# Shifted copies by small tile products and two heads' scores in the row halves of the array, in a ten-stage decoder kernel

## The chip, the cores and the metric

The kernel runs on one core of a Trainium2 chip. The metric is the device time in microseconds of one execution; the time before is the median of three runs. The profile is one further execution. TensorE (PE in the rows; PEld are its loads of weights), VectorE (DVE), ScalarE (ACT) and GpSimd (POOL) compute; SyncE (SP) only issues DMAs here. ScalarE issues a few DMAs too (ACTq in the rows).

## What is computed

256 tokens of 1024 features pass through four layers: a layer of two convolution mixers, a stick-breaking attention layer, each followed by a layer of 32 experts (top 2), and two layers of a second block (ab and nsa attention, a softmax with a bias by distance, each followed by a gated feed-forward and a small gated projection). What the change touches is cut out here:

```
g = b_val * sigmoid(b_gate)                     # 256 tokens x 512 channels
g = causal_depthwise_conv(g, conv_b_w)          # 31 taps, each channel on its own

z = einsum("bhqd,bhkd->bhqk", qb, kb) * scale   # 16 heads of 64, stick-breaking
log_keep = where(causal, log_sigmoid(-z), 0.0)
later = cumsum(log_keep, reverse=True) - log_keep
a = where(causal, exp(log_sigmoid(z) + later), 0.0)

s = einsum('bhqd,bhkd->bhqk', q, k) * ATTN_SCALE + bias   # ab and nsa, 16 heads of 64
p = softmax(where(mask, s, -inf));  o = p @ v
```

## The kernel before

One Python function writes all engines' programs in order; the order in the code is the order in each engine's queue. `later(n, f)` puts a piece of work `f` off by n ticks, and `tick()`, called after each half of a weight item, runs what is due. So attention work is strewn between the dense products.

Weights come as items of 1 MB through a stream of buffers: `pump` issues the next load on SP (L202) whenever a buffer is free, and `done` frees one. A dense product works in three float32r products (`mm3`, L397 to L399), for which each half of an item is split into a high part `wh` (ScalarE, L237) and a low part `wl` (VectorE, L248). A half of a `feat_unit` is 24 such products of 256 columns. The expert stages read their weights unsplit (L893, L915); they are 192 items each.

`conv_mix` is the first stage. It makes `gp` (two blocks of 128 channels, tokens along the row, with 30 zeros ahead), once per half i of the 512 channels. The 31-tap convolution is done by TensorE: row group s (32 rows) of `gs` holds the same 32 channels as the others, shifted by s tokens, so one product applies four taps, and eight products (q) of 32 output columns cover the taps. Four chunks c of 32 channels stand in the four column groups. `shifted(i)` makes `gs` from `gp` by a write to DRAM and four reads with a row offset, all issued by ScalarE (L607, L609). `conv(0)` follows the dense products of i = 1; `shifted(1)` comes directly behind it, and `conv(1)` after two more units.

In the stick-breaking stage a group of four heads is handled as two pairs m. `qz` holds the two heads of a pair in two planes r: plane 0 has head 0's 64 rows and zeros below, plane 1 zeros and head 1's rows, so one product with the pair's 128 rows of keys gives one head's scores. `scores` (L1126 to L1129; the helper `zmm` gives all of them line L1117) adds a causal mask by a product with an identity, `sums` adds the reversed cumulative sums by products with `ntri` and `nones`, `values` (L1167, L1170) multiplies by the values, 64 output columns per head. The ab stage (L1444, L1445) and the nsa stage (L1779, L1780, L1791, L1792) use such planes too, written by `put_q`. In nsa the product of the compressed values `vc` is L1808, 32 rows and 64 output columns per head.

Of the kernel before, what the change touches and what calls it, by code (L numbers as in the profile page):

```python
# [10 lines left out]
F32 = mybir.dt.float32  # L11
F32R = mybir.dt.float32r
# [8 lines left out]
SEQ = 256  # L21
# [49 lines left out]
def tile_kernel(ctx: ExitStack, tc: tile.TileContext, A, out, first=0, last=9):  # L71
# [468 lines left out]
    def conv_mix():  # L540


        with tc.tile_pool(name="cm", bufs=1, reuse_waits="tile") as cp:
# [84 lines left out]
            for i in range(2):  # L628
# [7 lines left out]
                shifted(i)  # L636
# [427 lines left out]
    def stick_mix():  # L1064
        with tc.tile_pool(name="st", bufs=1, reuse_waits="tile") as cp, \
# [14 lines left out]
            qz = cp.tile([128, 2, 2, SEQ], F32, name="qz")  # L1080
            G.memset(qz, 0.0)
# [37 lines left out]
            def attn(hg, qt, kt, vt):  # L1119
                st = {}  # L1120

                def scores(m):
                    z0, z1 = bank(), bank()
                    z0v = z0.rearrange("p (r t) -> p r t", r=2)
                    z1v = z1[:, 0:256].rearrange("p (r t) -> p r t", r=2)
                    zmm(z0v, kt[:, m, 0:128], qt[:, m], start=True)  # L1126
                    zmm(z0v[:, :, 0:128], identb, negb[:, None, :].to_broadcast([128, 2, 128]))
                    zmm(z1v, kt[:, m, 128:256], qt[:, m, :, 128:256], start=True)
                    zmm(z1v, identb, negb[:, None, :].to_broadcast([128, 2, 128]))  # L1129
                    sp = cw.tile([128, 768], F32, name="sp", bufs=3)  # L1130
                    for z, a, n in ((z0, 0, 512), (z1, 512, 256)):
                        S.activation(sp[:, a:a + n], z[:, 0:n], AF.Abs)
                    S.activation(sp, sp, AF.Exp, scale=-1.0)
                    S.activation(sp, sp, AF.Ln, bias=ones_t[:, 0:1])
                    for z, a, n in ((z0, 0, 512), (z1, 512, 256)):
                        V.scalar_tensor_tensor(sp[:, a:a + n], z[:, 0:n], 0.0, sp[:, a:a + n], op0=OP.max, op1=OP.add)
                    st[m] = (z0, z1, sp)

                def parts(m):
                    sp = st[m][2]  # L1140
                    sh = cw.tile([128, 768], F32R, name="sh")
                    S.activation(sh, sp, AF.Copy)
                    sl = cw.tile([128, 768], F32R, name="sl", tag="sp", bufs=3)
                    V.tensor_tensor(out=sl, in0=sp, in1=sh.bitcast(F32), op=OP.subtract)
                    st[m] = st[m][:2] + (sh, sl)

                def sums(m):
                    z0, z1, sh, sl = st[m]
                    z0v = z0.rearrange("p (r t) -> p r t", r=2)
# [5 lines left out]
                    a = cw.tile([128, 768], F32, name="a", tag="sp", bufs=3)  # L1155
                    S.activation(a[:, 0:512], z0, AF.Exp)
                    S.activation(a[:, 512:768], z1[:, 0:256], AF.Exp)
                    st[m] = a

                def values(m):  # L1160
                    a = st[m]
                    po = bank()
                    for i in range(2):
                        for r in range(2):
                            f = slice(m * 128 + r * 64, m * 128 + r * 64 + 64)
                            if i == 0:
                                T.matmul(po[64 * r:64 * r + 64, 0:256], vt[:, 0, f], a[:, r * 256:(r + 1) * 256],  # L1167
                                         start=True, stop=False)
                            else:
                                T.matmul(po[64 * r:64 * r + 64, 128:256], vt[:, 1, f],  # L1170
                                         a[:, 512 + r * 128:640 + r * 128], start=False, stop=True)
# [843 lines left out]
```

## Time and profile before

| | us |
|---|---|
| median of three runs | 1948.1 (1944.86 to 1948.65) |
| profiled execution | 1949.69 |
| its span | 1948.0 |
| TensorE busy in the span | 1646.1 (84%) |
| weight loads of TensorE busy | 1241.9 (64%) |
| VectorE busy | 741.1 (38%) |
| ScalarE busy | 676.2 (35%) |
| GpSimd busy | 125.7 (6%) |

The shares are means over stages with different limits, so the table alone names no bound. The stages, in the order of time, are conv (0 to about 150 us), experts (to 600), stick (to 731), experts (to 1190), ab (to about 1320), feed-forward and projection (to 1556), nsa (to 1716) and the second feed-forward and projection (to the end).

### The profile page before, as it was taken

How to read it: one execution, taken by the hardware profiler on the slowest of the kernel's cores; microseconds unless marked ns; L12 is line 12 of the kernel's file. 1: busy time of each engine (PE TensorE's matmuls, PEld its weight loads, DVE VectorE, ACT ScalarE, POOL GpSimd, SP SyncE). 2: the span in 40 equal slices, each digit the busy share in tenths (PEclk: the TensorE clock that was granted, in tenths of full speed). 3: DMA queues.
4: the chain of work that ended last, by engine and by line, in shares of the span. 5: the costliest groups of instructions: out<-in, count | busy, mean ns of one | idle time of the engine just before them, and what ended most of it. 6: DMA issues, size and time to landing. Idle time of an engine off the chain costs nothing. (4 is left out here: it accounts for less than half of the span.)

```text
span 1948.0 us, 34920 instructions
## 1 busy us (share of the span) xinstructions
PE 1646.1 (84%) x14941; PEld 1241.9 (64%) x14941; DVE 741.1 (38%) x1495; ACT 676.2 (35%) x1289; POOL 125.7 (6%) x130
## 2 busy tenths in 40 slices
PE   6799767668669999767658768999999998999998
PEld 6686323224226886323324235999999997799998
DVE  4163100001104663100001104666655857666557
ACT  3143112111114663211111114665444646654445
POOL 0001000000001000000000002111000412110002
PEclk9899877768788999878777788999999999999999
DMA  9659999999999649999999998545555463145550
GB/s 280 240 208 396 418 418 418 419 419 418 418 419 347 244 173 374 418 420 419 418 419 419 418 418 304 167 151 179 184 183 175 139 207 112 55 136 195 192 177 22
DMA packets 239033, 561.95 MB, mean 288 GB/s; under 512 B 15723, under 2 KB 127146, under 8 KB 238872
## 3 DMA queue, kind: packets, MB, share of 16 engines
q1 hardware_dynamic: 226520, 551.59, 74.3%
q10 hardware_dynamic: 11728, 7.88, 1.6%
q8 instruction: 120, 1.97, 0.4%
q14 instruction: 41, 0.34, 0.0%
q0 software_dynamic: 624, 0.18, 0.0%
HBM read 557.87 MB, written 1.74 MB: 287 GB/s over the span
## 5 line engine op out<-in xcount | busy, mean ns | idle before, releaser
L893 PE MATMUL ps<-w,xg 128*32 128x256 f32 x4096 | 365.7, 498 | 233.1 <-DMA w<-in_expert_w_up_dram 228.3
L893 PEld LDWEIGHTS ps<-w,xg 128*32 128x32 f32 x4096 | 136.4, 132 | 443.1 <-DMA w<-in_expert_w_up_dram 259.5
L248 DVE TENSOR_TENSOR wl<-w,wh 128x1024 fp32r<-128x1024 f32 x255 | 310.3, 1228 | 184.2 <-ACT wh L237 180.9
L237 ACT ACTIVATE wh<-w 128x1024 fp32r<-128x1024 f32 x273 | 282.9, 1051 | 102.2 <-PE ps L398 60.1
L897 DVE TENSOR_TENSOR hs<-hs,ps 128x128 f32<-128x128 f32 x64 | 18.4, 288 | 632.3 <-ACT hs L896 632.3
L397 PE MATMUL ps<-xh,wh 128*128 128x256 f32 (+1 forms) x840 | 237.5, 283 | 0.0
L399 PE MATMUL ps<-xh,wl 128*128 128x256 f32 (+1 forms) x840 | 236.7, 282 | 0.8 <-DVE wl L248 0.8
L398 PE MATMUL ps<-xl,wh 128*128 128x256 f32 (+1 forms) x840 | 236.9, 282 | 0.4 <-DVE xl L1219 0.3
L896 ACT ACTIVATE hs<-ps 128x128 f32<-128x128 f32 x64 | 17.7, 277 | 591.7 <-PE ps L893 587.1
L399 PEld LDWEIGHTS ps<-xh,wl 128*128 128x128 f32 (+1 forms) x840 | 159.4, 190 | 1.2 <-DVE wl L248 1.2
L398 PEld LDWEIGHTS ps<-xl,wh 128*128 128x128 f32 (+1 forms) x840 | 159.4, 190 | 1.2 <-DVE xl L1219 1.2
L397 PEld LDWEIGHTS ps<-xh,wh 128*128 128x128 f32 (+1 forms) x840 | 159.4, 190 | 0.0
L915 PE MATMUL ps<-w,ht 128*32 128x256 f32 x2048 | 145.3, 433 | 0.0
L922 ACT ACTIVATE y<-ps 32x256 f32<-32x256 f32 x256 | 95.8, 374 | 121.5 <-PE ps L915 114.2
L915 PEld LDWEIGHTS ps<-w,ht 128*32 128x32 f32 x2048 | 75.0, 129 | 68.8 <-issue 38.0
L399 PE MATMUL ps<-wh,xl 128*128 128x256 f32 x352 | 100.8, 286 | 5.0 <-DVE xl L1219 5.0
L248 POOL TENSOR_TENSOR wl<-w,wh 128x1024 fp32r<-128x1024 f32 x18 | 43.4, 2417 | 948.8 <-ACT wh L237 948.8
L397 PE MATMUL ps<-wh,xh 128*128 128x256 f32 x352 | 102.5, 291 | 1.5 <-ACT xh L1216 1.5
L398 PE MATMUL ps<-wl,xh 128*128 128x256 f32 x352 | 99.7, 283 | 0.0
L398 PE MATMUL ps<-al,wh 128*128 128x256 f32 x352 | 99.2, 282 | 0.0
L397 PE MATMUL ps<-ah,wh 128*128 128x256 f32 x352 | 99.2, 282 | 0.0
L399 PE MATMUL ps<-ah,wl 128*128 128x256 f32 x352 | 99.1, 282 | 0.0
(406 smaller groups left out, 2809.6 us busy)
## 6 DMA issues: line engine op xcount, KB each, us to landing
w<-in_expert_w_up_dram SPq DMA_DIRECT2D x256, 1024.0 KB, 17.9
w<-in_expert_w_down_dram SPq DMA_DIRECT2D x128, 1024.0 KB, 18.3
w<-in_w_ffn_gate_dram SPq DMA_DIRECT2D x22, 1024.0 KB, 5.7
w<-in_w_ffn_up_dram SPq DMA_DIRECT2D x22, 1024.0 KB, 5.3
w<-in_w_ffn_down_dram SPq DMA_DIRECT2D x22, 1024.0 KB, 4.9
w<-in_odd_w_qkv_dram SPq DMA_DIRECT2D x12, 1024.0 KB, 11.6
w<-in_w_in_ab_dram SPq DMA_DIRECT2D x12, 1024.0 KB, 9.5
w<-in_w_in_nsa_dram SPq DMA_DIRECT2D x10, 1024.0 KB, 5.3
```

The source lines that it names most:

```text
L237: S.activation(hv, src, AF.Copy)
L248: eng.tensor_tensor(out=lv, in0=src, in1=hv.bitcast(F32), op=OP.subtract)
L397: T.matmul(ps, lh, rh, start=start, stop=False, **kw)
L398: T.matmul(ps, lh, rl, start=False, stop=False, **kw)
L399: T.matmul(ps, ll, rh, start=False, stop=stop, **kw)
L893: T.matmul(pu[32 * j:32 * j + 32, 0:256], r, w[:, kk, :, j, :], start=k == 0, stop=k == 7)
L896: S.activation(hs, pu[:, 0:128], AF.Silu)
L897: V.tensor_tensor(out=hs, in0=hs, in1=pu[:, 128:256], op=OP.mult)
L915: T.matmul(pd[32 * c:32 * c + 32, 0:256], hts[e][:, 32 * j:32 * j + 32], w[:, jj, c * 256:(c + 1) * 256], start=j == 0, stop=j == 3)
L922: S.activation(y4s[q][32 * ee:32 * ee + 32, c * 256:(c + 1) * 256], pd[32 * c:32 * c + 32, 0:256], AF.Copy)
```

## The change

`shifted` no longer goes through DRAM. Per block b of 128 channels, 16 products of 32 rows and 32 output columns with a 32x32 block of the identity move each 32-channel chunk c into each row group s of a bank of its own, shifted by s columns; four copies, two on ScalarE and two on VectorE, then bring the banks to `gs`. The first call is put off by one tick.

The scores of the two heads of a pair are made with 64 rows each: head 0 in rows 0 to 63 of the array, head 1 in rows 64 to 127, with outputs in two banks. `qz` and its memsets go; `qt` holds queries without zeros, and each engine writes 256 columns on 128 partitions in place of 512 on 64. In the stick stage the two banks are now one per head, so masks, sums and activations are cut 384 + 384 in place of 512 + 256.

```diff
-            def shifted(i):
-                t = dram.tile([128, 2, 32 + SEQ], F32, name=f"shifts{i}")
-                S.dma_start(t, gp)
-                for s in range(4):
-                    S.dma_start(gs[32 * s:32 * s + 32], t.rearrange("(c f) b u -> f b c u", c=4)[:, :, :, s:s + 28 + SEQ])
+            def shifted():
+
+                for b in range(2):
+                    ps = [bank()[:, 0:28 + SEQ] for _ in range(4)]
+                    for s in range(4):
+                        for c in range(4):
+                            f = slice(32 * c, 32 * c + 32)
+                            T.matmul(ps[c][32 * s:32 * s + 32], ident[f, f], gp[f, b, s:s + 28 + SEQ], start=True,
+                                     stop=True)
+                    for c in range(4):
+                        if c % 2:
+                            S.activation(gs[:, b, c, :], ps[c], AF.Copy)
+                        else:
+                            V.tensor_copy(gs[:, b, c, :], ps[c])
...
                 if i:
                     conv(0)
-                shifted(i)
+                    shifted()
+                else:
+                    later(1, shifted)
...
-                    z0, z1 = bank(), bank()
-                    z0v = z0.rearrange("p (r t) -> p r t", r=2)
-                    z1v = z1[:, 0:256].rearrange("p (r t) -> p r t", r=2)
-                    zmm(z0v, kt[:, m, 0:128], qt[:, m], start=True)
-                    zmm(z0v[:, :, 0:128], identb, negb[:, None, :].to_broadcast([128, 2, 128]))
-                    zmm(z1v, kt[:, m, 128:256], qt[:, m, :, 128:256], start=True)
-                    zmm(z1v, identb, negb[:, None, :].to_broadcast([128, 2, 128]))
...
+                    zs = [bank()[:, 0:384] for _ in range(2)]
+                    for lo in (0, 128):
+                        for r in range(2):
+                            q = slice(64 * r, 64 * r + 64)
+                            zmm(zs[r][:, 256:384] if lo else zs[r][:, 0:256], kt[q, m, lo:lo + 128], qt[q, m, lo:],
+                                start=not lo)
+                    for z in zs:
+                        zmm(z.rearrange("p (a t) -> p a t", a=3)[:, 0:3:2], identb,
+                            negb[:, None, :].to_broadcast([128, 2, 128]))
...
-                    for v in (sh, sl):
-                        zmm(z0, ntri, v[:, 0:512])
-                        zmm(z0v[:, :, 128:256], nones, v[:, 512:768].rearrange("p (r t) -> p r t", r=2),
-                            stop=v is not sh)
-                        zmm(z1[:, 0:256], ntri, v[:, 512:768], stop=v is not sh)
...
+                    for r in range(2):
+                        for v in (sh, sl):
+                            zmm(zs[r][:, 128:256], nones, v[:, r, 256:384])
+                            zmm(zs[r], ntri, v[:, r], stop=v is not sh)
...
+    def put_q(qt, ps, gcol):
+
+        S.activation(qt[:, 0, :], ps[:, 0], AF.Copy, scale=qgain[:, gcol:gcol + 1])
+        V.tensor_scalar(qt[:, 1, :], ps[:, 1], qgain[:, gcol:gcol + 1], None, op0=OP.mult)
+
+    def two_heads(qt, kt, n):
+
+
+        bk = [bank(), bank()]
+        for a, lo in ((0, 0), (n, 128)):
+            for r in range(2):
+                q = slice(64 * r, 64 * r + 64)
+                T.matmul(bk[r][:, a:a + n - lo], qt[q, 0:128] if lo else qt[q, 128:256], kt[q, lo:n],
+                         start=True, stop=True)
+        return bk
```

ScalarE's queue in the convolution stage, from the tap rows to the copies of conv(0), before (names as in the text; `scr` takes conv's result; line numbers of after are shifted by the change):

```order
L596 ACTIVATE wv<-vec 32x4x7 x2
L237 ACTIVATE wh<-w 128x1024 x2
L607 DMA shifts_366<-gp 128x576
L609 DMA gs<-shifts_366 32x8x284 x4
L237 ACTIVATE wh<-w 128x1024 x2
L631 ACTIVATE sg<-ps 128x512
L237 ACTIVATE wh<-w 128x1024 x2
L619 ACTIVATE scr<-ps,vec 128x256 x2
L607 DMA shifts_561<-gp 128x576
L609 DMA gs<-shifts_561 32x8x284 x4
```

The same stretch of ScalarE's queue now:

```order
L596 ACTIVATE wv<-vec 32x4x7 x2
L237 ACTIVATE wh<-w 128x1024 x2
L616 ACTIVATE gs<-ps 128x284 x4
L237 ACTIVATE wh<-w 128x1024 x2
L640 ACTIVATE sg<-ps 128x512
L237 ACTIVATE wh<-w 128x1024 x2
L628 ACTIVATE scr<-ps,vec 128x256 x2
L616 ACTIVATE gs<-ps 128x284 x4
```

Where five DMA issues stood, four copies out of TensorE's banks stand, and the splits behind them wait for those.

TensorE's queue at the first call of scores in the ab stage, before (`kT` are the keys of a pair, `qz` its queries in two planes; the dense products stand on both sides):

```order
L399 MATMUL ps<-wh,xl 128x256
L1444 MATMUL ps<-kT,qz 128x256
L1445 MATMUL ps<-kT,qz 128x128
L1444 MATMUL ps<-kT,qz 128x256
L1445 MATMUL ps<-kT,qz 128x128
L397 MATMUL ps<-wh,xh 128x256
```

The same place of TensorE's queue now:

```order
L399 MATMUL ps<-wh,xl 128x256
L1375 MATMUL ps<-kT,qt 128x256 x2
L1375 MATMUL ps<-kT,qt 128x128 x2
L397 MATMUL ps<-wh,xh 128x256
```

The two heads' products of equal length now stand next to each other, in two row halves; their number is the same.

TensorE's queue at the sums of a pair in the stick stage, now (`sh` and `sl` are the two parts of the softplus; before there were six products, of 512, 256 and 256 columns twice):

```order
L1126 MATMUL ps<-sh,none 128x128
L1126 MATMUL ps<-sh,ntri 128x384
L1126 MATMUL ps<-sl,none 128x128
L1126 MATMUL ps<-sl,ntri 128x384
L1126 MATMUL ps<-sh,none 128x128
L1126 MATMUL ps<-sh,ntri 128x384
L1126 MATMUL ps<-sl,none 128x128
L1126 MATMUL ps<-sl,ntri 128x384
```

There are eight products, four per head, with the same columns in all.

## Rows read from the trace of the kernel before

**Rows 1.** Windows by stage: length; busy PE, PEld, DVE, ACT, POOL; clock; DMA share, GB/s.
```profile
150.00:600.00 450.00, 326.14 (x3489) 155.63 (x3489) 45.90 (x150) 73.60 (x199) 6.03 (x11) 0.81 1.02 414
600.00:731.00 131.00, 128.08 (x940) 111.00 (x939) 82.73 (x113) 78.48 (x117) 8.67 (x13) 1.00 0.69 240
...
1210.00:1330.00 120.00, 118.83 (x969) 113.14 (x969) 82.17 (x208) 70.20 (x152) 16.62 (x12) 1.00 0.48 149
1556.00:1716.00 160.00, 150.14 (x1140) 132.45 (x1140) 101.11 (x367) 90.16 (x238) 36.66 (x27) 0.97 0.38 121
```
**Rows 2.** Waits of TensorE, 0 to 130 us: us in total, times, longest.
```profile
PE ps L616 <- DMA gs<-shifts: 10.6, 2, 7.8
```
**Rows 3.** Timeline of ScalarE: start, length, engine, line, operation, count, [idle before].
```profile
29.04 0.35 ACTq L607 DMA_DIRECT2D shifts<-gp  x1
34.90 2.68 ACTq L609 DMA_DIRECT2D gs<-shifts  x4
37.68 2.00 ACT L237 ACTIVATE wh<-w 128x1024 fp32r<-128x1024 f32 x2 [13.68 <-issue]
```
**Rows 4.** Timeline of TensorE's products, 34 to 92 us.
```profile
34.63 0.27 PE L399 MATMUL ps<-w,wl 128*128 128x256 f32 x1
38.79 0.53 PE L397 MATMUL ps<-w,wh 128*128 128x256 f32 x1 [3.88 <-ACT wh L237]
...
47.99 1.07 PE L616 MATMUL ps<-gs,w 128*32 128x256 f32 x16 [2.88 <-DMA gs<-shifts]
...
56.72 0.38 PE L397 MATMUL ps<-w,wh 128*128 128x256 f32 x1
...
66.00 0.28 PE L399 MATMUL ps<-w,wl 128*128 128x256 f32 x1
...
82.01 1.08 PE L616 MATMUL ps<-gs,w 128*32 128x256 f32 x8 [7.76 <-DMA gs<-shifts]
...
91.32 0.39 PE L397 MATMUL ps<-w,wh 128*128 128x256 f32 x1
```
**Rows 5.** Windows within conv(1): length, busy PE, granted clock, DMA share, GB/s.
```profile
82.00:86.60 4.60, 4.59 (x44) 0.50 0.05 20
87.00:91.00 4.00, 4.00 (x81) 1.00 0.00 0
```
**Rows 6.** Waits of SP's DMA queue, 0 to 170 us, the longest.
```profile
SPq L202 <- DVE wl L248: 63.6, 9, 27.4
```
**Rows 7.** Timeline of TensorE around the value products of a pair, stick stage.
```profile
652.53 0.28 PE L399 MATMUL ps<-wh,w 128*128 128x256 f32 x1
652.74 0.65 PE L1167 MATMUL ps<-a,vt 128*64 128x256 f32 x4
653.22 0.39 PE L1170 MATMUL ps<-a,vt 128*64 128x128 f32 x4
...
653.76 0.28 PE L398 MATMUL ps<-w,wh 128*128 128x256 f32 x1
```
**Rows 8.** Timeline of TensorE, first half of a pair's sums, stick stage.
```profile
645.11 0.40 PE L1117 MATMUL ps<-sh,ntri 128*128 128x512 f32 x1
645.34 0.28 PE L1117 MATMUL ps<-sh,none 128*128 128x256 f32 x1
645.46 0.28 PE L1117 MATMUL ps<-sh,ntri 128*128 128x256 f32 x1
```
**Rows 9.** Timeline of TensorE around a pair's scores, ab stage.
```profile
1227.47 0.59 PE L1444 MATMUL ps<-kT,qz 128*128 128x256 f32 x2
1227.90 0.38 PE L1445 MATMUL ps<-kT,qz 128*128 128x128 f32 x2
...
1228.89 0.28 PE L398 MATMUL ps<-wl,xh 128*128 128x256 f32 x1
```
**Rows 10.** Timeline of TensorE, a pair's product with the compressed values, nsa stage.
```profile
1670.80 0.65 PE L1808 MATMUL ps<-pct,vc 32*64 32x256 f32 x4
```
**Rows 11.** Chain of work that ended last, products of one column.
```profile
1558.27 1.24 PE ps L1238 x12
```

More of the change, by code (lines that the diff above doesn't have):

```diff
@@ L1155, in sums @@
-                    a = cw.tile([128, 768], F32, name="a", tag="sp", bufs=3)
-                    S.activation(a[:, 0:512], z0, AF.Exp)
-                    S.activation(a[:, 512:768], z1[:, 0:256], AF.Exp)
+                    zs, sh, sl = st[m]
+                    for r in range(2):
+                        for v in (sh, sl):
+                            zmm(zs[r][:, 128:256], nones, v[:, r, 256:384])
+                            zmm(zs[r], ntri, v[:, r], stop=v is not sh)
+                    a = cw.tile([128, 2, 384], F32, name="a", tag="sp", bufs=3)
@@ L1158, in sums @@
+                    for r in range(2):
+                        S.activation(a[:, r], zs[r], AF.Exp)
                     st[m] = a
@@ L1351, in turn_heads @@
         return ps.rearrange("p (m t) -> p m t", m=2)
-    def put_q(qz, ps, gcol):
-        S.activation(qz[0:64, :, 0, :], ps[0:64], AF.Copy, scale=qgain[0:64, gcol:gcol + 1])
-        V.tensor_scalar(qz[64:128, :, 1, :], ps[64:128], qgain[64:128, gcol:gcol + 1], None, op0=OP.mult)
+    def put_q(qt, ps, gcol):
[4 more added lines that the diff above has]
+        for a, lo in ((0, 0), (n, 128)):
+            for r in range(2):
+                q = slice(64 * r, 64 * r + 64)
+                T.matmul(bk[r][:, a:a + n - lo], qt[q, 0:128] if lo else qt[q, 128:256], kt[q, lo:n],
+                         start=True, stop=True)
+        return bk
     def scaled_values(pool, ps, r, name, **kw):
@@ L1431, in ab_mix @@
                 tc.tile_pool(name="abw", bufs=2, reuse_waits="tile") as cw:
-            qz = cp.tile([128, 2, 2, SEQ], F32, name="qz")
-            G.memset(qz, 0.0)
+            qt = cp.tile([128, 2, SEQ], F32, name="qt")
             yh = bp.tile([128, 8, SEQ], F32R, name="yh", tag="qh")
@@ L1440, in scores @@
                     def scores(m=m):
-                        bk = []
-                        for r in range(2):
-                            sc = bank()
-                            T.matmul(sc[:, 0:256], qz[:, m, r, 128:256], kt[:, m, :], start=True, stop=True)
-                            T.matmul(sc[:, 256:384], qz[:, m, r, 0:128], kt[:, m, 128:256], start=True, stop=True)
-                            bk.append(sc)
-                        return bk
+                        return two_heads(qt[:, m, :], kt[:, m, :], 256)
                     def values(p, m=m):
@@ L1474, in turn_q @@
                 def turn_q(qn=qn, dil=dil):
-                    put_q(qz, turn_heads(qn, jdent, False), dil)
+                    put_q(qt, turn_heads(qn, jdent, False), dil)
                 later(4 if not hg else 3, turn_q)
@@ L1615, in nsa_mix @@
             pos, w2, b1, b2 = [sl[n] for n in ("pos", "w2", "b1", "b2")]
-            qz = [cp.tile([128, 2, 2, SEQ], F32, name=f"qz{i}") for i in range(2)]
-            for i in range(2):
-                G.memset(qz[i], 0.0)
+            qts = [cp.tile([128, 2, SEQ], F32, name=f"qt{i}") for i in range(2)]
             xh, xl = cur.h, cur.l
@@ L1763, in plan @@
             def plan(g, bias):
-                qt = qz[g % 2]
+                qt = qts[g % 2]
                 f = slice(g * 64, (g + 1) * 64)
@@ L1787, in win @@
                 def win(m):
-                    bk = []
-                    for r in range(2):
-                        sc = bank()
-                        T.matmul(sc[:, 0:256], qt[:, m, r, 128:256], kwt[:, g, :], start=True, stop=True)
-                        T.matmul(sc[:, 256:384], qt[:, m, r, 0:128], kwt[:, g, 128:256], start=True, stop=True)
-                        bk.append(sc)
+                    bk = two_heads(qt[:, m, :], kwt[:, g, :], 256)
                     if m == 0:
@@ L1855, in q_unit @@
                 qn, qs = head_norm(cw, tok_unit(xh, xl), cur, "qn")
-                return qs, lambda: put_q(qz[g % 2], turn_heads(qn, jdent, False), 2)
+                return qs, lambda: put_q(qts[g % 2], turn_heads(qn, jdent, False), 2)
             gate_unit()
```

43 lines of the change are left out of this document (16 added, 27 removed).

## The prediction

> **What bounds the kernel now.** I read the stages first, in the table of windows [rows 1]. The two expert stages are bound by the stream of weights: in 150 to 600 us the 16 DMA engines are busy all the time (share 1.02) while TensorE is busy 326 of 450 us. The three attention stages are bound by TensorE: 128.1 of 131 us busy in the stick-breaking stage (600 to 731), 118.8 of 120 in the ab stage, 150.1 of 160 in the nsa stage, with DMA shares of 0.69, 0.48 and 0.38. So whatever TensorE saves there moves the end, except where a wait already follows it.
>
> The convolution stage (0 to 150 us) is different, and I read it in three views: who TensorE waited for, the order of ScalarE's queue, and TensorE's timeline. TensorE waited 10.6 us in two places for the shifted copies `gs` [rows 2]. ScalarE's queue shows why more than that is lost [rows 3]. The write of `shifts` is issued at 29.04, the four reads of it only at 34.90 to 37.58, since they wait for the write to land, and they are issued by ScalarE: its next split of weights (L237) runs at 37.68, after 13.68 us in which it did nothing. TensorE's timeline [rows 4] has the consequence: the last product of a half at 34.63, the next only at 38.79; conv(0) starts at 47.99; conv(1) starts at 82.01, after 7.76 us of idle time. After such gaps the granted clock is low: 0.50 (the 1.2 GHz level) during the first half of conv(1), 1.00 during the second [rows 5].
>
> **Does time saved there reach the end?** The expert stage behind it is bound by its weights, so the question is what holds the weight stream before. SP's own waits in 0 to 170 us are mostly for `wl` of L248 (63.6 us in 9 waits) [rows 6]: it waits for buffers that the convolution stage has not yet used up. The stream is thus held by TensorE's progress, and if the stage ends X earlier, buffers come free X earlier, the stream becomes continuous X earlier, and the expert stage ends X earlier. I count X in full.
>
> **Part 1, the shifted copies.** Removed: five DMA issues per call of `shifted`, two calls, on ScalarE's queue; with them the round trip through DRAM. SP's queue loses nothing, but shares the DMA engines with them. Added: per call 32 products of 32x32 tiles over 284 columns on TensorE, four copies on ScalarE and four on VectorE. Moved: the first call by one tick, behind the first half of the next `feat_unit` (about 29 us), where `gp` is just written.
>
> What remains between 34.75 (34.63 and one product) and 91.32 when nothing waits: one half of 24 products at 0.117 us each (645.34 to 645.46, [rows 8]), 2.8 us; conv(0); the run from 56.72 to 66.12, 9.4 us, which never waited; another half, 2.8 us; conv(1). A conv at full clock is worth 7.0 us: 82.01 to 91.32 is 9.31 us, of which 4.65 up to 86.66 at half clock count as 2.3 [rows 4, 5]. Sum 2.8 + 7.0 + 9.4 + 2.8 + 7.0 = 29.0 us of 56.6, so 27.6 us are waits and low clock that the removal can give back.
>
> The new products are priced by bounds, since nothing in the trace runs sixteen tiles. conv's own products go four at a time: 64 of them in 7.0 us, 0.109 us each for 256 columns [rows 4, 5]; 32 of 284 columns would be 32 x 0.109 x 284/256 = 3.9 us a call. Sixteen at a time would be 1.0 us. The two products of `vc` (L1808) differ in row group and in column group, and their four passes lie within 0.65 us [rows 10], where one 256-column float32 product alone takes 0.43 us (1227.47 to 1227.90, [rows 9]): row groups do run together. I take 2.0 us a call, eight at a time, 4.0 us in all. By the Trainium skill (TensorE: Matmul & The Clock Gate, Measured speedup vs the span model) sixteen 32x32 tiles were 10.6 times as fast as one after the other; an estimate from that page is 1.5 us a call, and the sum would be 1 us lower. No row of this trace shows sixteen tiles.
>
> Cover of the rest: the eight copies of a call, shared by two engines, lie beside `feat_unit` in the first call and beside four halves (12 us) in the second; without that cover they would cost their own length, some 2 us a call. The first call waits for `gp`, written just before 29.04 [rows 3]; TensorE is there 48 products ahead of 34.75, at 29.1, so it waits 0.1 us or less. Next late is nothing that I see: of the two splits at 37.68 the first is of weights that TensorE wanted at 34.75, and ScalarE can make it as soon as its copies are done, at about 31. **Part 1: -27.6 + 4.0 = -23.6 us.**
>
> **Part 2, two heads in the row halves.** 32 calls of scores: 8 in stick, 8 in ab, 16 in nsa. Before, a call's products (256, 128, 256, 128 columns, heads padded with zeros to 128 rows) go one after the other: from 1227.47 to the normal pace behind (1228.89 less 0.12) 1.30 us [rows 9]. After, the same columns stand as two pairs. The trace has such pairs in other halves of the array: the value products L1167 and L1170, 64 output columns each, 256 + 128 columns per head. Between the normal pace ahead (652.65) and behind (653.76 less 0.12) they take 0.99 us [rows 7], though the columns of one head alone would be 0.64; the rest is the change of tile shape on both sides. So I take 0.31 us off per call. Bounds: 0.66 off if the switch costs nothing; 0.35 more than before if the pairs do not overlap and the switch is paid.
>
> The loads of weights may bind instead: a call still loads eight times, 128 columns wide, where the value products load 64. The row nearest to a bare load is L1238, 12 products of one column in 1.24 us [rows 11], 0.10 us each; eight in a line and the switch are 0.83 + 0.35 = 1.18 us, 0.12 off a call, and the sum 4 to 5 us higher, inside my range. The Trainium skill (TensorE: Matmul & The Clock Gate, LDWEIGHTS (loading the stationary operand)) speaks for that price: a load's time goes with its columns and not with its rows, so half-height loads save nothing. No row here shows a half-height load.
>
> Stick, per call of `sums`: 6 float32r products become 8, with the same 2048 columns. Before: 0.23, 0.12, 0.12 twice, 0.93 us [rows 8]. After: four of 384 columns (0.175) and four of 128. For 128 no row exists: half of 0.12 if columns count, 0.10 by the loads of [rows 11], 0.21 if such a short one goes at the float32 pace of [rows 9]. I take 0.10: 1.10 us, 0.17 more; the bounds are 0.0 and 0.6 more. Stick: 8 x (-0.31 + 0.17) = -1.1 us. Ab: 8 x -0.31 = -2.5 us. Nsa: 16 x -0.31 = -5.0 us, but TensorE already idles some 10 us there [rows 1], so part of what it saves only lengthens a wait for the softmax; I count half, -2.5 us. `put_q` writes half as many columns per engine, hidden by TensorE in stick and ab; the removed memsets are on GpSimd, which nobody waits for. **Part 2: -6.1 us.**
>
> **Sum.** -23.6 - 6.1 = -29.7. The profiled execution took 1949.7 us (span 1948.0), 1.6 more than the median 1948.1, so it becomes 1920.0 and the median **1918.4 us**.
>
> **Rivals.** (a) *Row groups do not run together; only column groups do.* Then a call of scores costs 0.35 more, `shifted` 3.9 a call: 27.6 - 7.8 = 19.8 won, 8 x 0.35 + 8 x (0.35 + 0.17) + 16 x 0.35 / 2 = 9.8 lost, 1938 us. For it: no row shows products that differ in row group alone. Against: L1808 [rows 10]. (b) *The tile products go one at a time,* in the order written, since neighbours share a column group: 64 x 0.109 x 4 x 284/256 = 31 us of TensorE in place of 27.6 us of waits, and the heads' 10 us: 1948 + 3 + 10 = 1961 us, **slower**. It decides from 0.43 us a product on (64 x 0.43 = 27.6). Against: conv itself overlaps four. (c) *The convolution stage's gain is swallowed by the weight stream:* the expert stage ends when the last weight lands, and if the stream were held by something other than buffers, only part 2 would be left: 1942 us. For it: share 1.02 from 150 us on. Against: SP waits for buffers [rows 6].
>
> **How the numbers follow.** Forecast 0.82, (a) 0.08, (b) 0.05, (c) 0.05. Within the forecast the low end takes sixteen tiles at a time (-25.6) and a free switch (8 x -0.66 twice and half of 16 x -0.66, -16): 1906. The high end takes four at a time (-19.8), the loads' price (0.12 off a call) and the dear 128-column products (8 x 0.6 more), +2: 1930. So 1906 to 1931, which leaves the three rivals out, 0.18. About 0.2% (4 us) is what a measurement of this kernel can tell from no change. Faster by more: forecast, (a) and (c), less a little for a mix of bad cases, 0.94; same 0.01; slower 0.05.
>
> **What would show it.** Right: no wait of TensorE for `gs`, no gap at 35 to 39 us, granted clock 1.00 from 12 us to the expert stage; conv(1) ending near 68 us; the products of `shifted` in about 2 us a call; the expert stage starting and ending some 24 us earlier with the same length; a call of scores in 1.0 us. Wrong: tile products whose starts lie 0.1 us or more apart; a longer first expert stage; new idle time in front of conv(1), where VectorE's copies stand ahead of its splits; `sums` well over 1.1 us.

## The result, and the profile after

The changed kernel takes **1918.97 us** (median of 4 runs, 1918.88 to 1923.46), the kernel before 1947.8 us beside it (4 runs, 1944.86 to 1948.65): a ratio of 0.9867, 95% interval 0.9852 to 0.9881 (the quotient of the two medians is 0.9852, at its lower end). The forecast was 1918.4 us. The profiled execution took 1918.91 us. Its page begins (span; busy time, share and instructions by engine):

```profile
span 1917.3 us, 35268 instructions
PE 1631.0 (85%) x15117; PEld 1228.9 (64%) x15117; DVE 738.6 (39%) x1503; ACT 676.8 (35%) x1297; POOL 122.0 (6%) x126
```

**Where the time went.** Some products stand at a border between stages in both kernels. Here they are in the trace of after (TensorE's timeline: start, length, engine, line, operation, count, idle before):

```profile
68.13 0.38 PE L397 MATMUL ps<-w,wh 128*128 128x256 f32 x1
...
580.63 0.33 PE L507 MATMUL ps<-ident,x 128*128 128x128 f32 x1 [0.49 <-DVE x L495]
...
704.65 0.38 PE L507 MATMUL ps<-ident,x 128*128 128x128 f32 x2
...
1165.42 0.33 PE L507 MATMUL ps<-ident,xn 128*128 128x128 f32 x1 [0.24 <-DVE xn L495]
...
1304.75 0.28 PE L1248 MATMUL ps<-ones_t,sq 128*128 128x1 f32 x2
...
1529.40 0.42 PE L1248 MATMUL ps<-ones_t,sq 128*128 128x1 f32 x2
...
1682.09 0.43 PE L1811 MATMUL ps<-pct,vc 32*64 32x256 f32 x2
```

The same products stand at 91.32 [rows 4], 605.60, 731.28, 1193.08, 1333.32, 1558.11 and 1713.55 us in the trace before. The differences, and what each stretch adds:

| up to the end of | before | after | earlier by | gained in the stretch |
|---|---|---|---|---|
| conv(1) | 91.32 | 68.13 | 23.2 | 23.2 |
| first expert stage | 605.60 | 580.63 | 25.0 | 1.8 |
| stick-breaking stage | 731.28 | 704.65 | 26.6 | 1.7 |
| second expert stage | 1193.08 | 1165.42 | 27.7 | 1.0 |
| ab stage | 1333.32 | 1304.75 | 28.6 | 0.9 |
| feed-forward between | 1558.11 | 1529.40 | 28.7 | 0.1 |
| nsa stage | 1713.55 | 1682.09 | 31.5 | 2.8 |
| span | 1948.0 | 1917.3 | 30.7 | -0.8 |

**The convolution stage.** Around the two calls of `shifted` and behind conv(1) TensorE's timeline reads:

```profile
29.29 2.18 PE L612 MATMUL ps<-gp,ident 32*32 32x284 f32 x64
...
31.40 0.39 PE L397 MATMUL ps<-w,wh 128*128 128x256 f32 x1
...
47.13 1.78 PE L612 MATMUL ps<-gp,ident 32*32 32x284 f32 x64
48.84 0.39 PE L397 MATMUL ps<-w,wh 128*128 128x256 f32 x1
...
67.80 0.40 PE L625 MATMUL ps<-gs,w 128*32 128x256 f32 x4
```

A call holds TensorE for 2.1 us (29.29 to 31.40) and 1.7 us; each float32 product is recorded as two passes, so 64 records are 32 products. As far as it has begun by 29.395 us, the first call reads:

```profile
29.29 0.52 PE L612 MATMUL ps<-gp,ident 32*32 32x284 f32 x16
```

Nothing of [rows 2] or of the gaps in [rows 4] is left. The granted clock in the two halves of conv(1), 0.50 and 1.00 in [rows 5] (columns as in [rows 1]):

```profile
61.00:64.50 3.50, 3.50 (x66) 2.11 (x68) 2.36 (x5) 0.91 (x2) 0.00 (x0) 1.00 1.03 405
64.50:68.20 3.70, 3.70 (x73) 2.02 (x61) 0.00 (x0) 0.00 (x0) 0.00 (x0) 1.00 0.91 363
```

ScalarE's queue, where [rows 3] showed 13.68 us without work, now has the copies (L616) and two splits of weights behind them:

```profile
30.26 0.71 ACT L616 ACTIVATE gs<-ps 128x284 f32<-128x284 f32 x2 [6.16 <-PE ps L612]
31.61 0.71 ACT L616 ACTIVATE gs<-ps 128x284 f32<-128x284 f32 x2 [0.64 <-PE ps L612]
32.20 2.00 ACT L237 ACTIVATE wh<-w 128x1024 fp32r<-128x1024 f32 x2
```

**The attention stages.** A call of scores in the ab stage, against [rows 9]:

```profile
1199.91 0.28 PE L399 MATMUL ps<-wh,xl 128*128 128x256 f32 x1
1200.12 0.92 PE L1375 MATMUL ps<-kT,qt 64*128 64x256 f32 x8
1200.97 0.39 PE L397 MATMUL ps<-wh,xh 128*128 128x256 f32 x1
1201.19 0.28 PE L398 MATMUL ps<-wl,xh 128*128 128x256 f32 x1
```

From the normal pace ahead (1199.91 + 0.12) to the normal pace behind (1201.19 - 0.12) it is 1.04 us in place of 1.30. The stick stage's sums, against [rows 8], come in four pairs of 128 and 384 columns:

```profile
619.45 0.22 PE L1126 MATMUL ps<-sh,none 128*128 128x128 f32 x1
619.51 0.39 PE L1126 MATMUL ps<-sh,ntri 128*128 128x384 f32 x1
619.74 0.22 PE L1126 MATMUL ps<-sl,none 128*128 128x128 f32 x1
...
620.60 0.28 PE L397 MATMUL ps<-wh,w 128*128 128x256 f32 x1
```

A call takes 1.15 us (619.45 to 620.60) where it took 0.93. A pair takes 0.285 us: 0.06 until the second product starts, 0.225 until the next pair.

### The profile page after: what moved, and what is told of

Its sections match the earlier page's. It is cut to its first block, busy times and chain, and to the rows that moved or that the text cites. A ratio compares the mean times of both kernels' runs of the same rounds, so it can differ in the third digit from the quotient of the medians.

```text
span 1917.3 us, 35268 instructions
## 1 busy us (share of the span) xinstructions
PE 1631.0 (85%) x15117; PEld 1228.9 (64%) x15117; DVE 738.6 (39%) x1503; ACT 676.8 (35%) x1297; POOL 122.0 (6%) x126
## 3 DMA queue, kind: packets, MB, share of 16 engines
HBM read 555.55 MB, written 1.15 MB: 290 GB/s over the span
## 5 line engine op out<-in xcount | busy, mean ns | idle before, releaser
L397 PE MATMUL ps<-xh,wh 128*128 128x256 f32 (+1 forms) x840 | 237.1, 282 | 0.0
L397 PEld LDWEIGHTS ps<-xh,wh 128*128 128x128 f32 (+1 forms) x840 | 159.3, 190 | 0.0
L397 PE MATMUL ps<-wh,xh 128*128 128x256 f32 x352 | 103.1, 293 | 1.5 <-ACT xh L1226 1.5
L248 POOL TENSOR_TENSOR wl<-w,wh 128x1024 fp32r<-128x1024 f32 x18 | 43.4, 2416 | 942.3 <-ACT wh L237 463.4
L397 PE MATMUL ps<-ah,wh 128*128 128x256 f32 x352 | 99.1, 281 | 0.0
```

The lines of the kernel that those rows point to most:

```text
L248: eng.tensor_tensor(out=lv, in0=src, in1=hv.bitcast(F32), op=OP.subtract)
L397: T.matmul(ps, lh, rh, start=start, stop=False, **kw)
```

## The experiments

All ratios are against the kernel before, run on the same chip (medians 1946.9 to 1947.2 us in these comparisons).

### Each part alone: copies_by_dram and heads_padded

```diff
-                    shifted()
-                else:
-                    later(1, shifted)
+                shifted(i)
...
+                t = dram.tile([128, 2, 32 + SEQ], F32, name=f"shifts{i}")
+                S.dma_start(t, gp)
```

> The shifted copies go through DRAM again, by ScalarE's queue, at their old place; the heads stay in the row halves. My theory (the two parts add up; in the trace of after the convolution stage ends 23.2 us earlier, and 25.0 us stand at the end of the first expert stage): 1919 + 25 = 1944 us (1941 to 1946), with TensorE waiting about 10 us for gs again. Rival: the heads give less than the attention stages seem to show (5.5 us there), because part of it is drift of the expert stages: then 1946 to 1948, no different from the kernel before.

Measured: 1940.82 us, ratio 0.9970 (0.9958 to 0.9982). TensorE's waits from 28 to 92 us (us in total, times, longest):

```profile
PE ps L616 <- DMA gs<-shifts: 8.2, 2, 5.3
PE ps L397 <- ACT wh L237: 6.3, 2, 3.8
```

```diff
-                        return two_heads(qt[:, m, :], kt[:, m, :], 256)
+                        bk = []
+                        for r in range(2):
+                            sc = bank()
+                            T.matmul(sc[:, 0:256], qz[:, m, r, 128:256], kt[:, m, :], start=True, stop=True)
+                            T.matmul(sc[:, 256:384], qz[:, m, r, 0:128], kt[:, m, 128:256], start=True, stop=True)
+                            bk.append(sc)
+                        return bk
```

The same stands in the nsa stage, and the stick stage has the scores and sums of the kernel before.

> The copies are made by tile products; the heads are padded with zeros to 128 rows as before. My theory: the attention stages are 5.5 us longer again, 1919 + 5.5 = 1924.5 us (1922 to 1927), and a call of scores takes 1.30 us from normal pace to normal pace in place of 1.04. Rival: the two gains overlap (a part of the heads' gain is taken from a wait that is also gone by the copies): 1920 or less.

Measured: 1926.71 us, ratio 0.9903 (0.9881 to 0.9925).

In its trace a call of scores takes 1.30 us again (1204.70 to 1206.00).

So the copies alone give 20.3 us by the medians and the heads alone 6.2; put on top of the other part they give 21.9 (1940.8 to 1919.0) and 7.7. Neither rival held: the heads alone are faster than no change, and the heads' gain does not vanish with the copies. 1926.7 lies in its range; 1940.8 lies just under its own, 1941 to 1946. The two gains alone add up to 26.5 us, both together to 28.8; each interval reaches 2 to 4 us to either side, so the parts add up as far as these runs can tell.

### Queue or latency: dram_by_gpsimd and dram_kept_warm

The round trip through DRAM held ScalarE's queue and it delayed `gs`. The first experiment takes only the queue away: in the kernel before, the five issues of a call go to GpSimd.

```diff
-                S.dma_start(t, gp)
+                G.dma_start(t, gp)
                 for s in range(4):
-                    S.dma_start(gs[32 * s:32 * s + 32], ...
+                    G.dma_start(gs[32 * s:32 * s + 32], ...
```

> The kernel before, with the five DMA issues of a call moved from ScalarE's queue to GpSimd's; the round trip through DRAM stays. If the loss in the convolution stage is ScalarE's blocked queue alone (splits of weights that come late, and the low clock after that): nearly all of the 23 us come back, 1925 us. If it is the latency of gs alone: no change, 1948 us. My theory is a mixture: the gap at 35 to 39 us and ScalarE's 13.7 us without work go, while conv(0) and conv(1) still wait some 5 us each for gs, with a low clock behind each wait; about 12 us come back, 1936 us (1930 to 1942).

Measured: 1940.58 us, ratio 0.9967 (0.9957 to 0.9977). TensorE's waits from 28 to 92 us, and GpSimd's issues on its timeline:

```profile
PE ps L616 <- DMA gs<-shifts: 9.3, 1, 9.3
PE ps L616 <- issue: 3.4, 1, 3.4
```

```profile
31.02 0.81 POOL L607 DMA_DIRECT2D shifts<-gp  x1 [28.58 <-DVE gp L633]
37.27 2.46 POOL L609 DMA_DIRECT2D gs<-shifts  x4 [5.44 <-DMA shifts<-gp]
```

The gap at 35 to 39 us is gone, and yet conv(0) starts at 48.55 us, not earlier than the 47.99 of [rows 4]: 31.02 to 48.55 is the round trip, 17.5 us where it was 19.0 before (29.04 to 47.99), beside a stream of weights that keeps the 16 DMA engines busy (share 1.07 from 36 to 48.5 us). The write is issued 2.0 us later than in the kernel before; 1.4 of that is a low clock at the start of this execution (see the last section). TensorE reached conv(0) earlier and waited longer. Only in the second call did the free queue help: conv(1) starts at 72.71 us in place of 82.01. In all 6.5 us came back by the medians, 8.7 at the end of conv(1) by the traces (82.65 against 91.32), some 10 if the late start is allowed for. So of the 23 us between a third and a little under a half went with the change of queue, and the rest is the round trip itself, with the low clock behind it. The share is not a clean one: the copies of GpSimd's queue also went in other packets (800 in place of 2464, for the same 2.92 MB from 28 to 90 us). The median is inside the range of the mixture, though its 12 us were too high; the theory of the queue alone is out. The Trainium skill (DMA: Bandwidth & Descriptors, Issuing engines are not separate DMA queues) says that issuing from another engine saves the sequencer's time and no transfer time; the 17.5 us against 19.0 agree in the main.

The second keeps the DRAM copies of copies_by_dram and fills TensorE's waits with idle products, to tell the low clock from the waits.

```diff
+                    warm(12)
                     conv(0)
                 shifted(i)
+                later(2 + i, lambda: warm(12))
...
+                    warm(24)
                     conv(1)
```

> As copies_by_dram, with idle products (512 columns, about 0.21 us each) put where TensorE waited: 12 ahead of the third half behind each call of shifted, 12 ahead of conv(0), 24 ahead of conv(1); they fill waits of 3.8, 2.9, 2.6 and 5.3 us. It tells the low clock behind the waits from the waits themselves. My theory: the clock stays at 1.00; both convs take 7.1 us in place of 8.8 and 9.8, which is 4.4 us at the end, while what the halves save is taken by a longer wait for gs, since its landing does not move: 1940.8 - 4.4 = 1936 us (1934 to 1939). Rival (all of the half-clock time counts, some 10 us): 1931 us. Rival (the clock costs nothing beside the waits): 1941 us.

Measured: 1938.70 us, ratio 0.9962 (0.9949 to 0.9975); the interval overlaps that of copies_by_dram, so this one is **inconclusive**. In its trace (an execution of 1945.2 us) conv(0) ran at full clock, 7.1 us long (8.8 in the kernel before), but `gs` of the second call landed later, 5.94 us behind the filling products, and the clock fell all the same (the window's columns as in [rows 1]):

```profile
83.70 0.66 PE L616 MATMUL ps<-gs,w 128*32 128x256 f32 x4 [5.94 <-DMA gs<-shifts]
```

```profile
83.00:89.00 6.00, 5.30 (x52) 2.97 (x56) 0.00 (x0) 0.00 (x0) 0.00 (x0) 0.50 0.01 2
```

What the low clock alone cost in the kernel before stays open.

### Does time in the convolution stage reach the end? extra_work

```diff
                 if i:
                     conv(0)
+                    warm(56)
                     shifted()
```

> The kernel after, with 56 idle products of 512 columns (bf16, about 0.21 us each, 11.9 us) on TensorE ahead of the second call of shifted, in the convolution stage. My theory (the weight stream is held by buffers that this stage uses up): the whole delay reaches the end, 1919 + 12 = 1931 us (1928 to 1933), the first expert stage starts and ends 12 us later. Rival (the first expert stage is held by the stream of weights from the start, and the convolution stage has room): 1919 to 1922 us.

Measured: 1933.79 us, ratio 0.9935 (0.9914 to 0.9957), 14.8 us over the kernel after. The products, and the first product behind the first expert stage:

```profile
48.18 12.26 PE L393 MATMUL ps<-onesb 128*128 128x512 bf16 x56
...
594.48 0.33 PE L507 MATMUL ps<-ident,x 128*128 128x128 f32 x1 [0.49 <-DVE x L495]
```

The products held TensorE for 12.2 us (to 60.37), and a low clock at the start of this execution cost 1.1 more (see the last section): 13.2 us in front of the expert stage (first L507 at 132.92 in place of 119.70), and 594.48 - 580.63 = 13.85 us behind it. The delay passes in full; the rival with room in the convolution stage is out. The median lies 0.8 us over the range of the expectation. At the end this execution is 15.9 us behind that of the kernel after: another 1.6 us came at the start of the stick stage, again with a low clock that the edit has no part in (last section).

### Which tiles run together: full_rows and full_rows_turned

```diff
-                            T.matmul(ps[c][32 * s:32 * s + 32], ident[f, f], gp[f, b, s:s + 28 + SEQ], start=True,
+                            T.matmul(ps[c][32 * s:32 * s + 32], ident[:, f], gp[:, b, s:s + 28 + SEQ], start=True,
```

> The 32 products of a call of shifted read all 128 rows (a 128x32 slice of the identity), so that neighbours differ in column group alone; the output is the same. My theory (sixteen tiles run together now, four then, at the 0.121 us a product that the convolution's own products show): a call's products take 3.9 us of streaming in place of about 0.7, and both calls together 5 to 6 us more, 1919 + 6 = 1925 us (1923 to 1927). Rival (a call's 2.1 and 1.7 us are waits for banks and not streaming, which four at a time would hide): 1919 to 1921 us. Rival (row groups give nothing): 1919 us.

Measured: 1935.40 us, ratio 0.9934 (0.9917 to 0.9951). The expectation misread the loop: the inner loop runs over `c`, so neighbours share the column group `s`, and with full rows nothing parts them: one product starts 0.48 us behind the other (30.51, 31.02, 31.49), two passes of 0.24. Since the first product of the next column group starts at 31.50, before the four are through, a call took 9.0 us, 0.28 a product on the mean. The next run exchanges the loops, so that neighbours do differ in column group:

```diff
-                    for s in range(4):
-                        for c in range(4):
+                    for c in range(4):
+                        for s in range(4):
```

> As full_rows (128 rows read per product), with the two loops of a block exchanged, so that neighbours in the queue write different column groups, as in the convolution itself; the output is the same. My theory: four run at a time, 0.121 us a product (0.109 x 284/256), 3.9 us a call in place of the 9.0 us of full_rows and the 2.1 and 1.7 us of sixteen tiles: 1919 + 4 = 1923 us (1921 to 1926). Rival (products that read all rows go one at a time whatever the column group, 0.28 us each): 1935 us, as full_rows.

Measured: 1923.50 us, ratio 0.9885 (0.9869 to 0.9902). The first call of `shifted` in full_rows (as far as it has begun by 30.80 us, then as a whole) and in full_rows_turned:

```profile
30.51 0.67 PE L612 MATMUL ps<-gp,ident 128*32 128x284 f32 x2
30.51 9.01 PE L612 MATMUL ps<-gp,ident 128*32 128x284 f32 x64
```

```profile
31.49 4.04 PE L612 MATMUL ps<-gp,ident 128*32 128x284 f32 x64
```

32 products take 4.0 us, as the convolution's own pace said (3.9). Read together: neighbours that share a column group go one after the other when they also share the rows (by 30.80 us only the two passes of one product have begun), while in the kernel after, in the same order but with 32 rows each, sixteen start within 0.10 us (29.29 to 29.39). So **row groups do run together**, and since column groups do too (4.0 us), all 16 tiles run at once.

### Pairs of heads: head_by_head and products_twice

```diff
-        for a, lo in ((0, 0), (n, 128)):
-            for r in range(2):
+        for r in range(2):
+            for a, lo in ((0, 0), (n, 128)):
```

The stick stage's scores are turned in the same way.

> The four score products of a call go head by head (256 and 128 columns of the first, then of the second) in place of pair by pair. My theory (the two row halves run together only where neighbours in the queue lie in different halves): only the first head's 128 columns can still run beside the second head's 256, so 0.21 us more per call, 1.25 in place of 1.04; 32 calls, half absorbed in the last attention stage: 1919 + 5 = 1924 us (1922 to 1929; the upper end if nothing overlaps). Rival (a call costs the change of tile shape and the loads of weights, the overlap gives nothing): 1919 us, 1.04 us a call.

Measured: 1921.92 us, ratio 0.9864 (0.9848 to 0.9881), no different from the kernel after by the intervals, and just under the range of the theory. A call reads, first as a whole, then as far as it has begun by 1205.60 and by 1206.095 us:

```profile
1205.55 0.93 PE L1375 MATMUL ps<-kT,qt 64*128 64x256 f32 x8
1206.41 0.39 PE L397 MATMUL ps<-wh,xh 128*128 128x256 f32 x1
```

```profile
1205.55 0.49 PE L1375 MATMUL ps<-kT,qt 64*128 64x256 f32 x2
```

```profile
1205.55 0.81 PE L1375 MATMUL ps<-kT,qt 64*128 64x256 f32 x5
```

The rival's number is right, but not its reason. By 1205.60 both heads' products of 256 columns run, 13 ns apart (7 in the kernel after, where they are neighbours), although the first head's 128 columns stand between them in program order; these, the fifth record, start at 1206.09. A product that waits for its own row half does not hold up the one behind it. The overlap is there in either order.

```diff
-        for a, lo in ((0, 0), (n, 128)):
+        for a, lo in ((0, 0), (0, 0), (n, 128), (n, 128)):
...
-                    for s in range(4):
+                    for s in (0, 1, 2, 3, 0, 1, 2, 3):
```

> Every new tile product runs twice: each pair of score products in the attention stages that two_heads serves, and the 16 products of each block of shifted; nothing else changes. My theory: a call of two_heads grows by the columns of one head alone, 0.64 us (0.43 + 0.21), from 1.04 to 1.68; a call of shifted by 32 products of 0.47 us, sixteen at a time, 0.95 us. Rival (the pairs go one after the other and the loads of weights hide): 1.28 us more a call. Rival (loads bind, 0.10 us each): 0.8 us more. For shifted: 1.9 us more at eight at a time, 3.9 at four. In sum 1919 + 5 + 5 + 2 = 1931 us.

Measured: 1934.73 us (one run), 15.8 over the kernel after where 12 were expected. A call of scores with all its products twice:

```profile
1205.87 1.58 PE L1375 MATMUL ps<-kT,qt 64*128 64x256 f32 x16
1207.38 0.39 PE L397 MATMUL ps<-wh,xh 128*128 128x256 f32 x1
```

The call grew by 0.66 us (1.51 from its first product to L397, against 0.85 in the kernel after): the columns of one head alone. So two heads cost what one costs, loads do not bind (0.8), and of the call's 1.04 us the remaining 0.38 do not grow with the products. I put them down to the change of tile shape, which the next experiment bears out. The records of a call place them: the first product starts 0.09 us later than the normal pace, its first pass is 0.10 longer than the second, and the first two products of normal shape behind are 0.09 and 0.10 late. The Trainium skill (TensorEngine Tiling (Array Packing), Key Properties) says that a change of tiling mode drains the array; it gives no price, and here it is these 0.38 us for both changes of a call, if all of them are that. In `shifted` the first call grew by 1.4 us (3.62 long in place of 2.18), between the 0.95 of sixteen at a time and the 1.9 of eight. The second call grew by 2.6 us (48.53 to 52.85 in place of 47.13 to 48.84); 1.0 of it is idle time ahead of the very last pass, and neither that nor the rest is traced.

### Two attempts at a faster version: side_by_side and small_waits

```diff
-                    later(1 + n, t.a)
+                    later(1 + (hg < 3), t.a)
                     later(2 + n, t.b)
                     later(4 + n, t.c)
-                    later(5 + n, t.d)
+                    later(8 if hg < 3 else 5 + n, t.d)
...
-                for j, f in ((i, "a"), (i - 1, "b"), (i - 2, "c"), (i - 3, "d")):
+                for j, f in ((i, "a"), (i - 3, "d"), (i - 1, "b"), (i - 2, "c")):
```

The stick stage's two score calls of a group also go into one tick.

> The kernel after, with tile-shaped products put next to each other: both score calls of a group of heads in one tick in the stick and ab stages, the ab stage's value products in the tick of the next group's scores, and in the nsa stage a step's value products straight behind its scores, ahead of the transposes. My theory (of a call's 1.04 us some 0.40 are the change of tile shape on both sides, and neighbours of tile shape share it): 3 to 4 changes saved per group in ab (4 x 3 x 0.35 = 4 us), one per step in nsa (16 x 0.35, half of it absorbed: 3 us), little in stick (the mask products stand between): 1919 - 7 = 1912 us (1908 to 1917). Rival (the cost is a start and an end for every group of one tensor, whatever the neighbour, or the softmax comes too late for the new places): 1919 us or more.

Measured: 1927.71 us, ratio 0.9893 (0.9876 to 0.9909): 8.7 us slower than the kernel after. Two neighbouring calls, a wait in the ab stage, and the longest wait of the nsa stage:

```profile
1207.80 1.58 PE L1375 MATMUL ps<-kT,qt 64*128 64x256 f32 x16
1209.31 0.39 PE L397 MATMUL ps<-wh,xh 128*128 128x256 f32 x1
...
1219.81 0.39 PE L398 MATMUL ps<-wl,xh 128*128 128x256 f32 x1 [0.41 <-DVE wl L248]
```

```profile
PE ps L1442 <- ACT pT L1432: 11.1, 5, 5.9
```

The change of shape is indeed shared: two calls take 1.70 us together (two apart: 2.08). But VectorE now has two calls' work in front of a split of weights, and TensorE waits for `wl` three times in the stick stage (0.5 us each) and three times in the ab stage (0.4 us each), where the kernel after waits once; in the nsa stage the value products come before the softmax is ready and wait 11.1 us for `pT`, which takes the place of the kernel after's 10.3 us for `sS` and `sM`. Between the products of the table above, the stick stage is 4.7 us longer than in the kernel after, the ab stage 0.3 and the nsa stage 3.1, so nothing of what was shared arrived. The second rival held, in its second half: the softmax and the splits come too late for the new places. A low clock, which the edit has no part in (last section), cost this profiled execution 2.5 us at the start and 1.5 of the 4.7 in the stick stage; the waits for `wl` are another 1.5, and the rest of the 4.7 and of the 3.1 I have not traced.

```diff
-                    later(1, shifted)
+                    later(1, lambda: shifted(0))
+                    later(2, lambda: shifted(1))
...
+                warm(6)
                 ps = bank()
```

The idle products stand in `vecs`, ahead of TensorE's first wait for a small load.

> The kernel after, with the second block of each call of shifted one tick later (four banks wanted at a time in place of eight) and six idle products in TensorE's first wait for a small load, 1.3 to 2.8 us long, behind which the granted clock fell to 0.50 for 3.4 to 6.8 us in most of the profiled executions of this study. My theory: about 0.5 us less per call, and 1.3 us less on average at the start: 1919 - 2 = 1917 us (1914 to 1919). Rival (one more change of tile shape per call eats the first, the idle products delay the loads' users): 1919 to 1921 us.

Measured: 1920.45 us, ratio 0.9867 (0.9851 to 0.9884): the same as the kernel after, and over the range of 1914 to 1919. A block alone takes

```profile
29.68 0.76 PE L612 MATMUL ps<-gp,ident 32*32 32x284 f32 x32
```

so two blocks are 1.5 us and not 2.1, 0.5 us less in the convolution stage, too little to be told from no change. Behind the idle products the granted clock stayed at 1.00 in the profiled execution, as it did in five of the twelve without them, so this run does not show what they are worth. No version of the study beats the kernel after.

## Why the prediction was right, point by point

By the table above the stages that were changed gave 23.2 + 1.7 + 0.9 + 2.8 = 28.6 us, where 29.7 were forecast; the stretches between them, which the edit does not touch, gave another 2.1 in this one trace. The mechanism held, but that the median came within 0.6 us of the forecast is luck: the interval of the ratio is 5.6 us wide, and the attention stages' terms below were off by 0.3 to 1.6 us, in both directions.

- **The shifted copies, 27.6 us of waits and low clock less 4.0 for the products, 23.6:** measured 23.2 at the end of conv(1), which ended at 68.13 us (68 forecast), at a granted clock of 1.00 throughout. The two calls cost 3.8 us. The choice of eight tiles at a time gave the right sum for a wrong reason: sixteen run at a time (a block of sixteen in 0.76 us), and the rest of a call is a wait in its second block, whose last banks, by the row below, come free only with the copies of the first; blocks a tick apart (small_waits) do not have it. That term was missing, and it made up for the price that was too high. The loads of weights in the first call show the wait:

```profile
30.71 0.22 PEld L612 LDWEIGHTS ps<-gp,ident 32*32 32x32 f32 x26 [0.58 <-ACT gs L616]
```

- **"ScalarE's queue shows why more than that is lost":** the step that was argued too strongly, though no number hung on it. dram_by_gpsimd gives 6.5 to some 10 of the 23 us to the queue; the larger part was the round trip, with the DMA engines full of weights meanwhile (share 1.07).
- **Passing to the end in full:** right, by extra_work; SP's waits for `wl` [rows 6] are still there, 56.7 us in 9 waits up to 147 us. The first expert stage was to keep its length; it is 1.8 us shorter in this trace (119.70 to 580.63, against 142.92 to 605.60). Over the thirteen profiled executions of this case that stretch lay between 460.9 and 463.4 us whatever the edit, with the kernel after at the low end: scatter, not a gain. The copies also left the DMA engines, with 2.92 MB; that gave nothing more that these traces show, since from the end of conv(1) to the expert stage it is 51.6 us in both (91.32 to 142.92 and 68.13 to 119.70).
- **A call of scores, 0.31 us off:** measured 0.26. The bound by a load's price (0.12 off) is out, and the half-height loads do not add up one after the other: products_twice adds 0.66 us for eight loads and their products, less than eight loads in a line (0.8).
- **The stick stage's sums, 0.17 more:** measured 0.22. The 128-column product was priced at 0.10 us; the next product starts 0.06 behind it, but the 384 columns then take 0.225 start to start where 0.175 was counted. Perhaps the short product does not cover the load of weights behind it; no run tests that.
- **Stick -1.1, ab -2.5, nsa -2.5:** measured -1.7, -0.9, -2.8. The ab stage's eight calls did save 2.1 us, but 0.6 us went to a longer wait for VectorE's `kn` (1.1 us for 0.5) and another 0.6 I have not traced. (Between the same two products it is 138.9 to 139.3 us in the traces in which the calls of this stage have half rows and their old places, and 140.2 to 140.4 with padded heads, so the saving lies between 0.9 and 1.5.) In the nsa stage 16 x 0.26 = 4.2 us were saved and 2.8 arrived; the wait for the softmax took the rest, as counted, though a third where a half was taken: TensorE's wait for `sS` there is

```profile
PE ps L1431 <- DVE sS L1424: 8.4, 3, 5.3
```

  against 6.8 us before. products_twice shows it from the other side: of 16 x 0.66 = 10.6 us put into that stage, 5.2 stand at its end (157.9 us between the two products of the table, against 152.7).
- **The rivals.** (a), row groups do not run together: out, by full_rows against the kernel after. (b), tile products one at a time: out; full_rows came nearest to it (its neighbours do go one after the other, at the 0.48 us that (b) took, but column groups overlap in part: 9.0 us a call), and even that stayed 12 us under the kernel before. (c), the gain swallowed by the weight stream: out, by extra_work.

## What to carry to other kernels

A round trip through DRAM that only rearranges a tile took 17.5 to 19 us here, for 288 KB out and four times 284 KB back beside a stream of weights (what it takes on idle DMA engines no run shows). Products with slices of the identity do the same in 0.76 us of TensorE a block, with copies on engines that had time for them. Look first at whether the stage's time passes to the end, by asking which queue waits for whom, and only then at what an operation costs. Work of an odd tile shape cost about 0.4 us per interruption here, but moving it together did not pay, since the softmax and the splits of weights came too late for it.

## What the runs showed of the hardware that I had not expected

- **Products pass a waiting one.** In head_by_head a product started 0.52 us before one that precedes it in program order (1205.57 and 1206.09 us); its own half of the array was free, that of the other was not. The Trainium skill (TensorE: Matmul & The Clock Gate, The mechanism) has matmuls start strictly in program order; for tiles this trace shows otherwise. In full_rows the next column group's first product started with the third of the four before it (31.49 and 31.50 us), so one waiting product was passed there, and two were not.
- **The clock behind a short wait differs from execution to execution.** Behind TensorE's first wait for a small load (L586, for `scr`) the granted clock fell to 0.50 for 3.4 to 6.8 us in seven of the thirteen profiled executions, and stayed at 1.00 in the others. It goes largely with the length of the wait: 1.5 to 2.8 us in the seven, 1.0 to 1.4 in five of the others, but 2.4 in the kernel before, where the clock stayed. At the start of the stick stage the wait (L409) is 1.9 us in every execution, and yet the clock fell behind it in five of the thirteen (extra_work, small_waits, side_by_side, dram_by_gpsimd and dram_kept_warm). What decides it no run shows. The same stretch in extra_work and in the kernel after:

```profile
20.00:23.00 3.00, 3.00 (x16) 3.00 (x15) 2.35 (x9) 2.89 (x9) 0.00 (x0) 0.50 0.13 21
```

```profile
20.00:23.00 3.00, 2.58 (x24) 2.41 (x22) 2.33 (x9) 2.90 (x9) 0.00 (x0) 1.00 0.15 21
```

  At the start it cost 1.1 to 2.6 us where it happened, the longer wait counted in, and in the stick stage 1.5 to 1.6, as much as several of the terms above; a single trace does not tell an edit of that size.
